# A two-layer hybrid trunk in float32: every dense product in passes of 256 columns at one distance of 180 bytes, decay rows on 128 partitions, block inverses written row by row

## The chip, the cores and the metric

The kernel runs on one core of a Trainium2 chip. The metric is the device time of one execution in microseconds, here the median of three runs. Where a single row is read, it comes from one profiled execution, whose span is a little shorter than the timed runs.

## The reference

The input `x` is 256 tokens of 2048 features, float32. Two layers follow one another, each a mixer and a gated feed-forward with residuals:

```python
# layer 0 mixer: differential attention, 8 heads, two score maps each
qkv = rms_norm(x) @ w_qkv            # 2048 -> 6144
p   = softmax(q k^T - slope * |i - j|)   # q, k normalised per head; chunk mask
x   = x + rms_norm((p1 - lam * p2) @ v) @ w_o
# layer 1 mixer: gated delta rule, 16 key heads, 32 value heads, chunks of 64
q, k, v = silu(causal_conv4(rms_norm(x) @ w_in)); z, beta, g from the same product
a   = I + strict_lower((k * beta) k^T * decay)   # per chunk and head
u   = a^-1 (v * beta); w = a^-1 (k * beta * exp(g))
o_t = q state + (q k^T * decay) (u - w state); state carried from chunk to chunk
x   = x + (rms_norm(o) * silu(z)) @ w_out
# both layers: feed-forward, 5504 hidden columns
u   = causal_conv3(rms_norm(x) @ w_up) + b
x   = x + (silu(gate(u)) * val(u)) @ w_down
```

## The kernel before

Tokens lie on the free axis: `x` and the normalised input `h` are 16 tiles of 128 features by 256 tokens. A float32 operand of a dense product is split into a rounded part and a rest, both of the type `float32r`: `h[k]` holds the two parts side by side (512 columns), and `weights` brings a chunk of four 128x256 weight tiles by DMA from the SP queue into `raw`, has ScalarE round it into `whi` (L89) and VectorE form the rest `wlo` (L90). Three buffers of each rotate. A product is then high x high, low x high and high x low, summed in PSUM.

`dense` does this with the weights as the loaded operand and the activations as the moving one. A step is one 128x128 weight tile and one of the two 128-column halves of the block. By default (L122 to L124) a step has three matmuls of 256 columns each. With `pair=True` it has two: `whi` against both parts of `h` in one matmul of 512 columns (L119), and `wlo` against the first part (L120); the two halves of the 512 columns are added later, in `merge` (L131 to L133) or by a second addition in `add_out` (L243). `pair` holds for the up-projections of both layers (43 blocks of 16 k x 2 steps each, `ffn`) and for the down-projection of layer 0 (8 blocks of 43 x 2 steps, `project`). All others use the default: queries, keys and `w_o` in layer 0, `w_in`, `w_gate` and `w_out` in layer 1, and the last down-projection. `dense_tok` (L148 to L150) has the roles exchanged: activations are loaded and 512 weight columns move. It makes the values of layer 0 (4 blocks) and `z` of layer 1 (8 blocks), each 96 matmuls.

The address at which `whi` and `wlo` start inside their buffers can be shifted by up to 127 elements (`weights(ap, d)`), so that the moving operand and the loaded one stand at a chosen distance modulo 512 bytes. `HP`, `AP` and `OP` are the places of `h`, `ac` and `oc` in such a row of 128 elements. The default products use a distance of 45 elements (180 bytes); the paired ones use one that changes with the block, and `dense_tok` one from the list `TOK`.

Small work is written as generators (`spawn`, `tick`) and mixed between the chunks; the framework's scheduler then sets the order on each engine. In the delta rule (`gdn`) there are four bands of four key heads. For each value head `keys` spreads a row of the decay over 128 partitions by a matmul of `sel` with `rows` on 64 partitions (L486). `invert` computes the inverses of the 32x32 diagonal blocks of a band on VectorE, all 128 partitions at once, into `Ti`, and turns them with two 32x32-block transposes into `ttc` (L543) and `tcc` (L545), laid out as element by matrix (`[partition, i, m]`). `levels` joins them to 64 and 128 rows: GpSimd copies them into `TT` and `Ta` (L558, L560), and TensorE multiplies 32x32 quadrants (L564 with `tcc`, L573 with `ttc`, then L577), twice a band. The trace has two records for each of these float32 matmuls.

Of the kernel before, what the change touches and what calls it, by code (L numbers as in the profile page):

```python
# [8 lines left out]
F32 = mybir.dt.float32  # L9
F32R = mybir.dt.float32r  # L10
# [12 lines left out]
TOK = [x for x in range(64) if x % 4 or x > 32 and x not in (32, 48)]  # L23
# [4 lines left out]
class Trunk:  # L28
# [49 lines left out]
    def weights(self, ap, d=(0, 0)):  # L78
# [8 lines left out]
        raw, hi, lo = tile_("raw", F32, 3), tile_("whi", F32R, 3, P, d[0]), tile_("wlo", F32R, 3, P, d[1])  # L87
# [13 lines left out]
    def dense(self, w, kt, acts, place, tiles=2, lead=0, dist=(45, 45), pair=False):  # L101

# [5 lines left out]
        for k0, nk in self.chunks(kt, CK, lead):  # L108
            hi, lo = self.weights(w[:, k0:k0 + nk, :], [(place - x) % P for x in dist])
# [3 lines left out]
            for k, c in steps:  # L113
# [4 lines left out]
                if pair:  # L118
                    nc.tensor.matmul(ps[:, c, :], hi[:, k, s], a, start=first, stop=False)  # L119
                    nc.tensor.matmul(o, lo[:, k, s], a[:, 0, :], start=False, stop=last)  # L120
                    continue
# [6 lines left out]
    def merge(self, ps, u, pair=False):  # L128

        if pair:  # L130
            self.nc.scalar.copy(u, ps[:, :, T:])  # L131
            self.nc.vector.tensor_tensor(u, ps[:, :, :T], u, ALU.add)
# [4 lines left out]
    def dense_tok(self, w, kt, acts, dists):  # L137
# [3 lines left out]
        for i, (k0, nk) in enumerate(self.chunks(kt, CK // 2)):  # L141
# [97 lines left out]
    def add_out(self, blk, ps, done, pair=False):  # L239

        x = self.x[:, 2 * blk:2 * blk + 2, :]
        for i in range(1 + pair):
            self.nc.vector.tensor_tensor(x, ps[:, :, i * T:(i + 1) * T], x, ALU.add)  # L243
# [5 lines left out]
    def project(self, w, kt, acts, place, done, final=False, pairs=None):  # L249

        n = KD // 2
        for b in range(n):
            ps = self.dense(w[b], kt, acts, place, dist=pairs[b] if pairs else (45, 45), pair=bool(pairs))
            if b < n - final:
                self.add_out(b, ps, done, bool(pairs))
                continue
# [5 lines left out]
    def ffn(self, w_up, w_down, nj, cols_ap, done, final=False):  # L262
# [3 lines left out]
        with self.tc.tile_pool(name="fp", bufs=1) as fp:  # L266
# [5 lines left out]
            for j in range(nj):  # L272
                ps = self.dense(w_up[j], KD, self.h_acts, HP, dist=2 * ((j if not final else 43 + j if j < 21 else 3 * j - 60),), pair=True)
                c = []
                u = fp.tile([P, 2, T], F32, tag="u", name="u", bufs=2)
                self.merge(ps, u, True)
# [11 lines left out]
            self.project(w_down, nj, lambda k: acts[k], AP, done, final, None if final else [(53, 8), (58, 8), (53, 40), (58, 40), (12, 8), (53, 60), (58, 60), (53, 52)])  # L288

    def attention(self, w_qk, w_v, w_o, nh, dist_ap, ident_ap, qg, kg, lvec, sub, start, done, lambda_init):  # L290

        nc, mp = self.nc, self.mp
        with self.tc.tile_pool(name="at", bufs=1) as at:
# [115 lines left out]
            for h in range(0, nh, 2):  # L409
                pv = self.dense_tok(w_v[h // 2], KD, self.h_acts, TOK[2 * h:2 * h + 4])  # L410
# [12 lines left out]
    def gdn(self, w_gate, w_in, w_z, w_out, nb, hb, gate_ap, const_ap, hot_ap, conv_col, ng, done):  # L423
# [12 lines left out]
        with tc.tile_pool(name="gd", bufs=1) as gd:  # L436
# [4 lines left out]
            hot = gd.tile([64, nv], F32, tag="hot", name="hot")  # L441
# [27 lines left out]
            def keys(hq, c, cc, b0, res):  # L469
# [448 lines left out]
```

## Time and profile before

| | |
|---|---|
| time, median of 3 runs | 2720.66 us (2720.05 to 2721.29) |
| profiled execution: its own time is known by its span | 2716.8 us |
| TensorE busy | 2701.9 us (99%), 18912 matmuls |
| VectorE, ScalarE, GpSimd busy | 1909.1, 1489.6, 120.1 us |
| DMA | 481.18 MB, mean 177 GB/s |

By stage, the attention layer takes the first 401 us, the feed-forward of layer 0 lasts to 1125, the delta rule to 1994, the feed-forward of layer 1 to the end at 2717. Busy times are unions over overlapping instructions. Matmuls overlap, so a matmul's own duration is longer than the time that it adds; what it adds is the distance from its start to the next start. In the rows of groups the numbers after the bar are busy time and mean duration of one, then idle time before. In the timeline a row is start, duration, engine, line, operation and tiles (`out<-moving,loaded` for matmuls).

### The profile page before, as it was taken

What the parts mean: (1) busy time and instruction counts of PE and PEld (TensorE: products, weight loads), DVE (VectorE), ACT (ScalarE), POOL (GpSimd) and SP (SyncE); (2) the same over time, 40 slices, a digit from 0 to 9 for tenths busy, and PEclk for the clock granted to TensorE, in tenths of its full rate; (3) what the DMA queues carried; (4) which work ended last, traced back from release to release, by engine and by line L of the source; (5) the groups of instructions that cost most, each with busy time, mean ns of one, the idle gap of its engine ahead of it and who ended that gap; (6) DMA issues with size and microseconds to landing.
All of it is one profiled execution on the core that took longest, in us unless ns stands there. A gap on an engine that the chain in (4) does not pass through costs nothing.

```text
span 2716.8 us, 46973 instructions
## 1 busy us (share of the span) xinstructions
PE 2701.9 (99%) x18912; PEld 2474.2 (91%) x18912; DVE 1909.1 (70%) x2813; ACT 1489.6 (55%) x2077; POOL 120.1 (4%) x220
## 2 busy tenths in 40 slices
PE   8999999999999999999999999999999999999999
PEld 8998898888888888889989989989998888889999
DVE  7775667777777555679687687688677777776444
ACT  6665555555555444574564664574565555555333
POOL 0000000000000000022011011021000000000000
PEclk9999999999999999999999999999999999999999
DMA  6555566666666666655355454455466666666665
GB/s 207 172 171 171 158 200 188 187 190 189 187 187 189 188 189 186 183 158 182 117 162 170 131 169 150 153 164 166 143 193 186 187 188 189 188 188 191 204 200 167
DMA packets 135370, 481.18 MB, mean 177 GB/s; under 512 B 15344, under 2 KB 18416, under 8 KB 135152
## 3 DMA queue, kind: packets, MB, share of 16 engines
q1 hardware_dynamic: 134000, 475.57, 57.9%
q8 instruction: 148, 2.42, 0.4%
q10 hardware_dynamic: 1152, 2.61, 0.3%
q14 instruction: 70, 0.57, 0.1%
HBM read 476.03 MB, written 2.10 MB: 176 GB/s over the span
## 4 chain that ended last, share of the span: by engine, by line
PE 99%; DMA 0%; ACT 0%; DVE 0%; issue 0%; SPq 0%; DVEq 0%; ACTq 0%
PE ps L119 29%; PE ps L120 15%; PE ps L123 13%; PE ps L122 12%; PE ps L124 12%; PE ps L149 3%; PE ps L150 3%; PE ps L148 3%; PE mp L621 2%; PE mp L236 1%; PE mp L509 1%; PE mp L564 0%; PE mp L573 0%; PE mp L486 0%; PE mp L585 0%; PE mp L591 0%
## 5 line engine op out<-in xcount | busy, mean ns | idle before, releaser
L90 DVE TENSOR_TENSOR wlo<-raw,whi 128x1024 fp32r<-128x1024 f32 (+2 forms) x909 | 1108.5, 1221 | 661.5 <-ACT whi L89 658.8
L89 ACT CAST whi<-raw 128x1024 fp32r<-128x1024 f32 (+2 forms) x909 | 947.8, 1043 | 1030.1 <-PE ps L119 430.0
L119 PE MATMUL ps<-h,whi 128*128 128x512 f32 x2752 | 964.9, 394 | 0.0
L120 PE MATMUL ps<-h,wlo 128*128 128x256 f32 x2752 | 772.8, 281 | 0.0
L119 PEld LDWEIGHTS ps<-h,whi 128*128 128x128 f32 x2752 | 516.8, 188 | 120.6
L120 PEld LDWEIGHTS ps<-h,wlo 128*128 128x128 f32 x2752 | 518.3, 188 | 0.0
L122 PE MATMUL ps<-h,whi 128*128 128x256 f32 x1552 | 433.1, 280 | 7.9 <-ACT h L162 5.9
L123 PE MATMUL ps<-h,wlo 128*128 128x256 f32 x1552 | 433.6, 280 | 2.0 <-DVE wlo L90 2.0
L124 PE MATMUL ps<-h,whi 128*128 128x256 f32 x1552 | 432.3, 279 | 0.0
L122 PEld LDWEIGHTS ps<-h,whi 128*128 128x128 f32 x1552 | 292.4, 189 | 10.3 <-ACT h L162 5.9
L123 PEld LDWEIGHTS ps<-h,wlo 128*128 128x128 f32 x1552 | 293.1, 189 | 5.6 <-DVE wlo L90 2.7
L124 PEld LDWEIGHTS ps<-h,whi 128*128 128x128 f32 x1552 | 293.1, 189 | 1.1
L122 PE MATMUL ps<-ac,whi 128*128 128x256 f32 x944 | 260.5, 276 | 0.0
L123 PE MATMUL ps<-ac,wlo 128*128 128x256 f32 x944 | 260.4, 276 | 0.0
L124 PE MATMUL ps<-ac,whi 128*128 128x256 f32 x944 | 260.3, 276 | 0.0
L119 PE MATMUL ps<-ac,whi 128*128 128x512 f32 x688 | 241.8, 395 | 0.0
L120 PE MATMUL ps<-ac,wlo 128*128 128x256 f32 x688 | 193.2, 281 | 0.0
L122 PEld LDWEIGHTS ps<-ac,whi 128*128 128x128 f32 x944 | 177.1, 188 | 0.1
L123 PEld LDWEIGHTS ps<-ac,wlo 128*128 128x128 f32 x944 | 177.1, 188 | 0.0
L124 PEld LDWEIGHTS ps<-ac,whi 128*128 128x128 f32 x944 | 177.1, 188 | 0.0
L119 PEld LDWEIGHTS ps<-ac,whi 128*128 128x128 f32 x688 | 129.5, 188 | 30.8
L148 PE MATMUL ps<-whi,h 128*128 128x512 f32 x384 | 152.8, 398 | 0.0
(211 smaller groups left out, 3418.2 us busy)
## 6 DMA issues: line engine op xcount, KB each, us to landing
raw<-w_up SPq DMA_DIRECT2D x344, 512.0 KB, 4.4
raw<-w_down SPq DMA_DIRECT2D x160, 512.0 KB, 3.8
raw<-w_in SPq DMA_DIRECT2D x128, 512.0 KB, 4.3
raw<-w_z SPq DMA_DIRECT2D x64, 512.0 KB, 3.7
raw<-w_out SPq DMA_DIRECT2D x64, 512.0 KB, 4.0
raw<-w_qk SPq DMA_DIRECT2D x63, 512.0 KB, 4.2
raw<-w_v SPq DMA_DIRECT2D x32, 512.0 KB, 3.6
raw<-w_o SPq DMA_DIRECT2D x32, 512.0 KB, 4.6
```

The source lines that it names most:

```text
L89: nc.scalar.copy(hi, raw)
L90: nc.vector.tensor_tensor(lo, raw, hi.bitcast(F32), ALU.subtract)
L119: nc.tensor.matmul(ps[:, c, :], hi[:, k, s], a, start=first, stop=False)
L120: nc.tensor.matmul(o, lo[:, k, s], a[:, 0, :], start=False, stop=last)
L122: nc.tensor.matmul(o, hi[:, k, s], a[:, 0, :], start=first, stop=False)
L123: nc.tensor.matmul(o, lo[:, k, s], a[:, 0, :], start=False, stop=False)
L124: nc.tensor.matmul(o, hi[:, k, s], a[:, 1, :], start=False, stop=last)
L148: nc.tensor.matmul(ps[:, c, :], ah, hi[:, k, :], start=first, stop=False)
L149: nc.tensor.matmul(ps[:, c, :], ah, lo[:, k, :], start=False, stop=False)
L150: nc.tensor.matmul(ps[:, c, :], al, hi[:, k, :], start=False, stop=last)
L236: last = self.nc.tensor.matmul(out, self.onesr, p[:, j], start=i + j == 0, stop=i + j == n)
L621: nc.tensor.matmul(p[:, v, :], l(v), r[:, v, :], start=i == 0, stop=i == len(terms) - 1)
```

## The change

Three things change.

1. `pair` is gone: every step of `dense` has three matmuls of 256 columns, and every dense product, `dense_tok` too, stands at a distance of 45 elements (`GAP`). In `dense_tok` each 512-column matmul becomes two of 256. `merge` loses two of its three operations in the paired form, `add_out` its second addition.
2. `sel` and the decay `rows` have 128 partitions, of which the upper 64 hold zeros (`hot` is padded with zeros on the way in, GpSimd clears `rows`).
3. `ttc` and `tcc` are laid out as matrix by element (`[partition, m, i]`): the transposes write at a stride, and the matmuls and GpSimd's copies read 32 elements in a row. In `levels` the loop over matrices is outside the loop over the quadrants 0 and 2.

```diff
-TOK = [x for x in range(64) if x % 4 or x > 32 and x not in (32, 48)]
+GAP = 45
...
-    def dense(self, w, kt, acts, place, tiles=2, lead=0, dist=(45, 45), pair=False):
+    def dense(self, w, kt, acts, place, tiles=2, lead=0):
...
-            hi, lo = self.weights(w[:, k0:k0 + nk, :], [(place - x) % P for x in dist])
+            hi, lo = self.weights(w[:, k0:k0 + nk, :], (place - GAP) % P)
...
-                if pair:
-                    nc.tensor.matmul(ps[:, c, :], hi[:, k, s], a, start=first, stop=False)
-                    nc.tensor.matmul(o, lo[:, k, s], a[:, 0, :], start=False, stop=last)
-                    continue
                 nc.tensor.matmul(o, hi[:, k, s], a[:, 0, :], start=first, stop=False)
                 nc.tensor.matmul(o, lo[:, k, s], a[:, 0, :], start=False, stop=False)
                 nc.tensor.matmul(o, hi[:, k, s], a[:, 1, :], start=False, stop=last)
...
-        if pair:
-            self.nc.scalar.copy(u, ps[:, :, T:])
-            self.nc.vector.tensor_tensor(u, ps[:, :, :T], u, ALU.add)
-            self.nc.vector.tensor_tensor(u, u, self.rstd.unsqueeze(1).to_broadcast([P, 2, T]), ALU.mult)
-            return
         self.nc.vector.tensor_tensor(u, ps[:, :, :T], self.rstd.unsqueeze(1).to_broadcast([P, 2, T]), ALU.mult)
...
-            hi, lo = self.weights(w[:, k0:k0 + nk, :], 2 * ((HP + dists[i // 2]) % P,))
+            hi, lo = self.weights(w[:, k0:k0 + nk, :], (HP + GAP) % P)
...
-                    nc.tensor.matmul(ps[:, c, :], ah, hi[:, k, :], start=first, stop=False)
-                    nc.tensor.matmul(ps[:, c, :], ah, lo[:, k, :], start=False, stop=False)
-                    nc.tensor.matmul(ps[:, c, :], al, hi[:, k, :], start=False, stop=last)
+                    halves = [slice(i * T, (i + 1) * T) for i in range(2)]
+                    for j, (l, r) in enumerate(((ah, hi), (ah, lo), (al, hi))):
+                        for i, s in enumerate(halves):
+                            nc.tensor.matmul(ps[:, c, s], l, r[:, k, s],
+                                             start=first and not (i or j), stop=last and i + j == 3)
...
-                    sel = gd.tile([64, P], F32R, tag="sel", name="sel", bufs=2)
-                    nc.gpsimd.tensor_copy(sel, hot[:, h:h + 1].to_broadcast([64, P]))
+                    sel = gd.tile([P, P], F32R, tag="sel", name="sel", bufs=2)
+                    nc.gpsimd.tensor_copy(sel, hot[:, h:h + 1].to_broadcast([P, P]))
...
-                nc.vector.transpose(ttc.rearrange(flat), t.rearrange(flat))
+                nc.vector.transpose(ttc.rearrange("p m i -> p i m"), t)
                 tcc = gd.tile([P, 32, 32], F32, tag="s4", name="tcc", bufs=3)
-                nc.vector.transpose(tcc, t.rearrange("p i c -> p c i"))
+                nc.vector.transpose(tcc.rearrange("p m c -> p c m"), t.rearrange("p i c -> p c i"))
...
-                    nc.gpsimd.tensor_copy(TT[quad[s], :, quad[s]], ttc[quad[s], :, ms].rearrange("p i m -> p m i"))
+                    nc.gpsimd.tensor_copy(TT[quad[s], :, quad[s]], ttc[quad[s], ms, :])
...
-                for s in (0, 2):
-                    for m in range(nm):
+                for m in range(nm):
+                    for s in (0, 2):
                         nc.tensor.matmul(pp[quad[s + 1], m, :], lview[m // 2][quad[s], m % 2, quad[s + 1]],
-                                         tcc[quad[s], :, m0 + m], start=True, stop=True)
+                                         tcc[quad[s], m0 + m, :], start=True, stop=True)
...
-        rows = gd.tile([64, T], F32R, tag="grow", name="grow")
-        nc.scalar.copy(rows, pr)
+        rows = gd.tile([P, T], F32R, tag="grow", name="grow")
+        nc.gpsimd.memset(rows[64:].bitcast(F32), 0.0)
+        nc.scalar.copy(rows[:64], pr)
```

Where the rows of an engine's queue change is best seen at three places. First TensorE, before the change, where layer 0's first up-projection block (`ps_4522`) follows the last block of `w_o` (`ps_4383`); a row is line, operation, out<-moving,loaded and size:

```order
L122 MATMUL ps_4383<-ac_3548,whi_4475 128x256
L123 MATMUL ps_4383<-ac_3548,wlo_4476 128x256
L124 MATMUL ps_4383<-ac_3548,whi_4475 128x256
L119 MATMUL ps_4522<-h_75,whi_4524 128x512
L120 MATMUL ps_4522<-h_75,wlo_4525 128x256
```

The same place after the change (the numbers of tiles differ between the two programs, and `dense`'s three matmuls are now lines 115 to 117):

```order
L115 MATMUL ps_4767<-ac_3932,whi_4859 128x256
L116 MATMUL ps_4767<-ac_3932,wlo_4860 128x256
L117 MATMUL ps_4767<-ac_3932,whi_4859 128x256
L115 MATMUL ps_4906<-h_75,whi_4908 128x256
L116 MATMUL ps_4906<-h_75,wlo_4909 128x256
L117 MATMUL ps_4906<-h_75,whi_4908 128x256
```

The up-projection now goes on in the same pattern as the block ahead of it. The second place is a burst of 32-row products of the third band on TensorE, before; `whi_17408` and `wlo_17409` are the two parts of one weight chunk:

```order
L122 MATMUL ps_17359<-h_75,whi_17408 128x256
L564 MATMUL mp_16876<-tcc_16850,lt_16002 32x32 x2
L564 MATMUL mp_16876<-tcc_16850,lt_16010 32x32 x2
L564 MATMUL mp_16876<-tcc_16850,lt_16187 32x32 x2
L564 MATMUL mp_16876<-tcc_16850,lt_16195 32x32 x2
```

And the same burst after, with the matmuls of two quadrants now side by side:

```order
L115 MATMUL ps_20290<-h_75,whi_20292 128x256
L553 MATMUL mp_19759<-tcc_19721,lt_18741 32x32 x4
L553 MATMUL mp_19759<-tcc_19721,lt_18749 32x32 x4
L553 MATMUL mp_19759<-tcc_19721,lt_18926 32x32 x4
L553 MATMUL mp_19759<-tcc_19721,lt_18934 32x32 x4
L116 MATMUL ps_20290<-h_75,wlo_20293 128x256
```

In both programs the burst stands behind the first matmul of a block's first chunk, whose rest part is the next that VectorE has to form. The third place is VectorE ahead of that burst, before:

```order
L539 TENSOR_TENSOR Ti_16565<-Ti_16565,tmp_16827 128x30
L543 STREAM_TRANSPOSE ttc_16848<-Ti_16565 128x1024
L545 STREAM_TRANSPOSE tcc_16850<-Ti_16565 128x1024
L90 TENSOR_TENSOR wlo_17409<-raw_17407,whi_17408 128x1024
L135 TENSOR_TENSOR u_17347<-ps_17154,rstd_11096 128x512
```

and after:

```order
L90 TENSOR_TENSOR wlo_20239<-raw_20237,whi_20238 128x1024
L207 SCALAR_TENSOR_TENSOR cv_20074<-u_20072,cols_79,cv_20074 128x253 x2
L532 STREAM_TRANSPOSE ttc_19719<-Ti_19316 128x32x32
L534 STREAM_TRANSPOSE tcc_19721<-Ti_19316 128x32x32
L90 TENSOR_TENSOR wlo_20293<-raw_20291,whi_20292 128x1024
```

The transposes keep their place between two weight splits; the split behind them, `wlo_17409` before and `wlo_20293` after, is the one that TensorE needs right behind the burst.

More of the change, by code (lines that the diff above doesn't have):

```diff
@@ L237, in total, with add_out @@
         return last
-    def add_out(self, blk, ps, done, pair=False):
+    def add_out(self, blk, ps, done):
         x = self.x[:, 2 * blk:2 * blk + 2, :]
-        for i in range(1 + pair):
-            self.nc.vector.tensor_tensor(x, ps[:, :, i * T:(i + 1) * T], x, ALU.add)
+        self.nc.vector.tensor_tensor(x, ps[:, :, :T], x, ALU.add)
         if done:
@@ L247, in add_out, with project @@
             self.add_squares()
-    def project(self, w, kt, acts, place, done, final=False, pairs=None):
+    def project(self, w, kt, acts, place, done, final=False):
         n = KD // 2
         for b in range(n):
-            ps = self.dense(w[b], kt, acts, place, dist=pairs[b] if pairs else (45, 45), pair=bool(pairs))
+            ps = self.dense(w[b], kt, acts, place)
             if b < n - final:
-                self.add_out(b, ps, done, bool(pairs))
+                self.add_out(b, ps, done)
                 continue
@@ L272, in ffn @@
             for j in range(nj):
-                ps = self.dense(w_up[j], KD, self.h_acts, HP, dist=2 * ((j if not final else 43 + j if j < 21 else 3 * j - 60),), pair=True)
+                ps = self.dense(w_up[j], KD, self.h_acts, HP)
                 c = []
                 u = fp.tile([P, 2, T], F32, tag="u", name="u", bufs=2)
-                self.merge(ps, u, True)
+                self.merge(ps, u)
                 for half in range(2):
@@ L570, in levels @@
                 px = small(32)
-                for s in (0, 2):
-                    for m in range(nm):
-                        nc.tensor.matmul(px[quad[s], m, :], pc[quad[s + 1], m, :], ttc[quad[s + 1], :, m0 + m],
+                for m in range(nm):
+                    for s in (0, 2):
+                        nc.tensor.matmul(px[quad[s], m, :], pc[quad[s + 1], m, :], ttc[quad[s + 1], m0 + m, :],
                                          start=True, stop=True)
@@ L843, in _layout @@
         "const": np.concatenate(const, 1).astype(f),
-        "hot": np.concatenate([np.eye(NV)] * 2).astype(f),
+        "hot": np.concatenate([np.eye(NV)] * 2 + [np.zeros((P - 2 * NV, NV))]).astype(f),
         "w_up1": blocks(x["ffn_w_up"][1], KD, up),
```

22 lines of the change are left out of this document (11 added, 11 removed).

## The prediction

> **What bounds the kernel now.** I read the page's head and its chain of waits first, then the list of TensorE's waits, then the busy time by stage.
>
> ```profile
> span 2716.8 us, 46973 instructions
> ...
> PE 99%; DMA 0%; ACT 0%; DVE 0%; issue 0%; SPq 0%; DVEq 0%; ACTq 0%
> ```
>
> ```profile
> PE ps L122 <- ACT h L162: 5.9, 1, 5.9
> PE ps L123 <- DVE wlo L90: 2.0, 3, 1.2
> PE ps L122 <- ACT whi L89: 2.0, 1, 2.0
> PE mp L730 <- DVE glin L726: 1.2, 1, 1.2
> ```
>
> The chain is TensorE at 99%, and TensorE waits 11.1 us in all (total, times, longest in each row), nearly all of it at the start and at the entry of the delta-rule layer. So the time is the sum of the distances from one matmul's start to the next one's, and the question is what each kind of matmul adds to that sum. A row's duration (276 to 400 ns) is no help, because matmuls overlap; starts and counts are. The stages of the two feed-forward layers give both. The windows below are up-projection of layer 0, its down-projection, up-projection of layer 1, its down-projection; the first number after the window is its length in us, then come TensorE's busy time and matmuls, its weight loads, VectorE, ScalarE, GpSimd, and last the granted clock, the DMA share and GB/s.
>
> ```profile
> 401.60:883.80 482.20, 482.20 (x2760) 422.39 (x2759) 362.89 (x518) 276.52 (x389) 0.00 (x0) 1.00 0.62 189
> 883.90:1125.50 241.60, 241.60 (x1377) 210.87 (x1376) 126.65 (x137) 101.99 (x121) 0.00 (x0) 1.00 0.63 183
> ...
> 1994.70:2478.80 484.10, 484.10 (x2760) 423.04 (x2759) 363.48 (x518) 276.34 (x389) 0.00 (x0) 1.00 0.62 188
> 2478.90:2712.70 233.80, 233.80 (x2065) 233.80 (x2064) 110.98 (x101) 90.74 (x91) 0.00 (x0) 1.00 0.66 193
> ```
>
> The two down-projections do the same arithmetic (8 blocks of 43 x 2 steps). The first does a step in a pass of 512 and a pass of 256 columns (1376 matmuls, 241.60 us, 351 ns a step); the last does it in three passes of 256 at 180 bytes (2064 matmuls, 233.80 us, 113.3 ns a pass, 340 ns a step). The clock column is 1.00 in all four. This pair is the main evidence: the form that the change brings everywhere is already there, 7.8 us shorter for the same work.
>
> **The change, part by part.**
>
> *Feed-forward steps.* 43 x 32 + 8 x 86 + 43 x 32 = 3440 steps take 482.20 + 241.60 + 484.10 = 1207.9 us. After it they are 10320 passes at 113.3 ns, 1169.2 us, and the 16 records of the norms inside the two up windows stay (a pass each, 1.8 us). Gain 36.9 us. The built program has moving minus stationary address at 180 modulo 512 bytes in every dense matmul, with the same buffers as before, so nothing but the passes differs from the last window. What goes with it on the other engines is off the path:
>
> ```profile
> L132 DVE TENSOR_TENSOR u<-ps,u 128x512 f32<-128x512 f32 x86 | 58.8, 684 | 0.0
> L131 ACT COPY u<-ps 128x512 f32<-128x512 f32 x86 | 49.9, 580 | 0.0
> ```
>
> Both go (as does one of two additions at `add_out` in layer 0's down-projection, 8 of some 0.69 us); the multiply by `rstd` stays and reads PSUM. I cost this at nothing, as TensorE has no row waiting for `u`. The cover that must hold is that weights keep up with shorter blocks: VectorE was busy 362.89 of 482.20 us in the first window and needs 43 x 0.68 less in about 469; DMA moved 193 GB/s in the last window, the pace now asked of the up windows, without a wait of TensorE. Would the cover go, up blocks would stay at some 350 ns a step and the 36.9 would shrink to the 7.7 of the down-projection.
>
> *Token-major products* (`dense_tok`: values in layer 0, `z` in the delta rule; 12 blocks of 96 passes of 512 columns become 192 of 256). Two stretches with nothing else on TensorE:
>
> ```profile
> 273.90:290.55 16.65, 16.65 (x75) 13.51 (x74) 10.37 (x14) 9.44 (x15) 0.00 (x0) 1.00 0.57 167
> ...
> 1816.80:1847.84 31.04, 31.04 (x135) 24.97 (x133) 27.31 (x52) 12.24 (x13) 3.22 (x8) 1.00 0.63 190
> ```
>
> Three of each count stand across the edges, so 16.65/72 = 231 and 31.04/132 = 235 ns a pass; I take 233.2. 1152 passes are 268.6 us. After: 2304 passes. No row has them, since here the weights move and the activations are loaded; the bounds are 113.3 (above) and 120 ns (rows further down). I take 113.3, as the moving address again lies 180 bytes above the loaded one and each pass again has one weight load: 261.0 us, gain 7.6 us (at 120: a loss of 7.9).
>
> *Decay rows.* `sel` x `rows` on 64 partitions, 32 times (one for each value head). Beside it, a 128-partition matmul of the same type among passes:
>
> ```profile
> 39.58 0.28 PE L123 MATMUL ps<-h,wlo 128*128 128x256 f32 x1
> 39.69 0.39 PE L236 MATMUL mp<-sqp,onesr 128*128 128x512 f32 x1
> 39.93 0.28 PE L124 MATMUL ps<-h,whi 128*128 128x256 f32 x1
> 40.04 0.28 PE L122 MATMUL ps<-h,whi 128*128 128x256 f32 x1
> ```
>
> ```profile
> 1171.80 0.28 PE L124 MATMUL ps<-h,whi 128*128 128x256 f32 x1
> 1172.01 0.38 PE L486 MATMUL mp<-grow,sel 64*128 64x256 f32 x1
> 1172.32 0.38 PE L122 MATMUL ps<-h,whi 128*128 128x256 f32 x1
> 1172.54 0.28 PE L123 MATMUL ps<-h,wlo 128*128 128x256 f32 x1
> ```
>
> The full-height one slips in at pass speed (39.58 to 40.04: two passes and twice 256 columns). The half-height one makes gaps of 0.21, 0.31 and 0.22 us around it: 0.74 us where three passes take 0.35. 32 x 0.39 = 12.5 us gained; the bounds are 0 (if the gaps have another cause) and 12.5, and I take the upper, since number type, columns and neighbours are alike and only the height differs. GpSimd's wider copies, the zeros in 64 rows and the larger `hot` load are off TensorE's queue; nothing waits for GpSimd there.
>
> *Block inverses.* The 32-row products read `tcc` and `ttc` at a stride of 32 elements, one row quadrant after the other; after, they read 32 elements in a row and alternate quadrants. Each of 8 bursts (4 bands, 2 groups):
>
> ```profile
> 1657.86 0.28 PE L122 MATMUL ps<-h,whi 128*128 128x256 f32 x1
> 1658.06 1.75 PE L564 MATMUL mp<-tcc,lt 32*32 32x32 f32 x32
> 1659.74 0.39 PE L123 MATMUL ps<-h,wlo 128*128 128x256 f32 x1
> ```
>
> ```profile
> 1287.69 1.58 PE L573 MATMUL mp<-ttc,pc 32*32 32x32 f32 x29
> ...
> 1289.10 0.23 PE L573 MATMUL mp<-ttc,pc 32*32 32x32 f32 x1
> 1289.11 0.22 PE L577 MATMUL mp<-pc,TT 32*32 32x32 f32 x2
> 1289.16 0.23 PE L573 MATMUL mp<-ttc,pc 32*32 32x32 f32 x1
> 1289.17 0.22 PE L577 MATMUL mp<-pc,TT 32*32 32x32 f32 x2
> ...
> 1289.23 0.51 PE L577 MATMUL mp<-pc,TT 32*32 32x32 f32 x11
> 1289.67 0.38 PE L122 MATMUL ps<-h,whi 128*128 128x256 f32 x1
> ```
>
> L564: first to last start 1.75 - 0.23 = 1.52 us for 32, 48 ns each. L577, contiguous on one quadrant: (0.51 - 0.19)/10 = 32 ns. Two quadrants at once (1289.10 to 1289.16): three starts in 60 ns, 20 each. I take 22, 0.70 us a burst, saving 0.8 x 8 = 6.6 us (at 32 ns: 4.0; at 16: 8.1). L573 with L577 behind it lasts 1.98 us (1287.69 to 1289.67); 0.70 + 16 x 0.032 + 0.12 = 1.33, saving some 0.6 x 8 = 4.9. Together 11.5 us, bounds 0 (stride and order cost nothing) and 14.6. The price is on VectorE, which writes these tiles:
>
> ```profile
> 1654.03 1.25 DVE L543 STREAM_TRANSPOSE ttc<-Ti 128x1024 f32<-128x1024 f32 x1
> 1655.20 2.09 DVE L545 STREAM_TRANSPOSE tcc<-Ti 128x1024 f32<-128x1024 f32 x1
> ```
>
> A strided input costs 0.84 us. Strided output has no row; if it costs as much, the first gets 0.84 longer and the second as much again. `tcc` ended at 1657.29, the burst began at 1658.06: 0.77 us of cover, and queued behind the transposes is the weight split for the next chunk. At most both double, +3.3 us, 2.5 beyond the cover in 4 bands: 0 to 10 us; I take 1 us, nearest to the strided-input row. GpSimd's copies into `TT` and `Ta` get contiguous reads and end no later. The scheduler moved a few bursts (rows of the order, above): I count three more interruptions by half- or quarter-height work, at the 0.2 us of such an entry (1657.86 to 1658.06), 0.5 us.
>
> *Sum.* 36.9 + 7.6 + 12.5 + 11.5 - 1.0 - 0.5 = 67.0 us, against the profiled span of 2716.8: 2649.8. The median of the runs is 2720.7, 3.9 above the span; with that, 2653.7 us. The 11.1 us of waits stay.
>
> **The rivals.** *A 256-column pass costs more than half of a 512-column one everywhere* (a fixed part per matmul, paid 4592 times more). For it speaks an up block of layer 1:
>
> ```profile
> 2030.13 0.39 PE L119 MATMUL ps<-h,whi 128*128 128x512 f32 x1
> 2030.36 0.28 PE L120 MATMUL ps<-h,wlo 128*128 128x256 f32 x1
> 2030.48 0.40 PE L119 MATMUL ps<-h,whi 128*128 128x512 f32 x1
> ```
>
> 0.12 after 0.23. At 118 ns a pass the feed-forward would take 11.7 us more and the token products 3.3 more; with the 22.5 of the other parts, 2713.2 us. Against it is the last window's 113.3. The Trainium skill ("TensorE: Matmul & The Clock Gate", section "Wait — 56ns, not 53.3ns?") speaks for this rival: it gives each warm matmul its columns over the clock plus a fixed 2.5 ns. By its figures three passes of 256 would be 2.5 ns longer than 512 + 256, an estimate of 11.5 us lost over 4592 splits, and about 2709.7 us; the windows disagree with it, 340 against 351 ns a step.
>
> *Slower: the passes fall into a slower rhythm.* Eight passes in the delta rule, no other work between:
>
> ```profile
> 1541.72 0.28 PE L124 MATMUL ps<-h,whi 128*128 128x256 f32 x1
> ...
> 1542.68 0.28 PE L123 MATMUL ps<-h,wlo 128*128 128x256 f32 x1
> ```
>
> 0.96/8 = 120 ns at the very same 180 bytes: there is a second rhythm, entered after other work. Should the up blocks enter it and stay, 10320 x 0.120 = 1238.4 us: 32.3 lost, 7.9 with the token products, 22.5 gained: 2738.4 us. It decides from (1207.9 + 268.6 + 22.5 - 1.8)/12624 = 118.6 ns a pass. Against it: the last window kept 113.3 for 234 us.
>
> *Only the token products* take 120: 2669.2. *Bursts no shorter*: 2665.2. *VectorE becomes the bound while it inverts* (27.31 of 31.04 us busy above, and longer transposes): up to 9 us more, 2662.7.
>
> **How the numbers follow.** The sum as worked out: 0.70, with a range of its own of 2646 to 2661 (bursts at their ends, transposes free or covered). Token products at 120: 0.09. Bursts no shorter: 0.07. VectorE: 0.05. Fixed part per matmul: 0.04. Slower rhythm: 0.03; 0.02 for what I don't see. 2643 to 2676 takes in all but the last three and leaves a little below for the slow rhythm leaving the delta rule. A measurement can tell about 0.2%, 5.4 us: faster 0.93 (the first four cases and half of the fixed part), within it 0.03 (the other half, where it meets bursts or token products that don't gain, and 0.01 unseen), slower 0.04 (the slow rhythm, 0.01 unseen).
>
> **What would show it.** Right: up windows near 469 us with 4136 matmuls, both down-projections alike at 234; token stretches at 113 ns; no gaps of 0.2 to 0.3 us around the `sel` matmul; 32-row bursts near 0.7 us; waits still near 11 us. Wrong: 118 to 120 ns in the up windows, rows of TensorE waiting for `wlo` or `tcc`, or bursts still at 48 ns a start.

## The result and the profile after

The changed kernel takes 2675.01 us (median of 4 runs, 2674.91 to 2676.33), the kernel before 2720.36 beside it (4 runs): a ratio of 0.983, interval 0.982 to 0.985. The forecast was 2653.7, in a range of 2643 to 2676: the direction and most of the steps were right, but 45 us came instead of 67, and the time lies 1 us inside the slow end of the range.

The profiled execution has a span of 2674.6 us (2716.8 before). These are the windows of the changed kernel by stage: attention, up- and down-projection of layer 0, the delta-rule layer, up- and down-projection of layer 1. The first number after the window is its length; the columns are those of the windows before.

```profile
0.00:405.20 405.20, 395.73 (x3296) 391.59 (x3297) 269.50 (x401) 236.59 (x379) 0.20 (x4) 1.00 0.57 178
405.20:874.00 468.80, 468.80 (x4137) 468.75 (x4136) 334.83 (x476) 256.65 (x347) 0.00 (x0) 1.00 0.64 194
874.00:1107.90 233.90, 233.90 (x2066) 233.90 (x2065) 121.66 (x129) 101.48 (x120) 0.00 (x0) 1.00 0.65 190
1107.90:1967.80 859.90, 855.03 (x7814) 842.50 (x7813) 672.98 (x1135) 511.94 (x711) 111.94 (x217) 1.00 0.52 160
1967.80:2436.60 468.80, 468.80 (x4137) 468.75 (x4136) 335.12 (x476) 256.43 (x347) 0.00 (x0) 1.00 0.64 194
2436.60:2670.50 233.90, 233.90 (x2066) 233.90 (x2064) 110.38 (x100) 90.25 (x90) 0.00 (x0) 1.00 0.67 193
```

The feed-forward layers gave what was forecast, 482.20 to 468.80, 241.60 to 233.90 and 484.10 to 468.80. What is missing is in the two other windows: the delta rule went from 868.9 to 859.9 us only, and attention got longer, 401.6 to 405.2. In attention 3.2 of these 3.6 us are the products of the values, 89.9 to 93.1 us, which were split like `z`.

What happened in the delta rule can be seen in two neighbouring stretches with almost nothing but passes in them. The first is the second `z` block (192 token-major passes), the second the two dense blocks behind it (2 x 96 passes):

```profile
1205.79:1228.83 23.04, 23.04 (x195) 23.04 (x193) 20.36 (x39) 9.57 (x10) 0.00 (x0) 1.00 0.61 194
1228.83:1251.87 23.04, 23.04 (x195) 23.04 (x193) 21.05 (x38) 10.91 (x13) 2.93 (x5) 1.00 0.52 161
```

23.04/192 = 120.0 ns a pass in both. The token products run at 120 and not at 113.3, which was one of the rivals. And the dense blocks behind, which have the distance of 180 bytes that gave 113.3 in the feed-forward layers, go on at 120 until other work interrupts them. The timeline of TensorE shows this at a burst of the third band:

```profile
1634.57 0.28 PE L117 MATMUL ps<-h,whi 128*128 128x256 f32 x1
1634.69 0.28 PE L115 MATMUL ps<-h,whi 128*128 128x256 f32 x1
1634.90 0.69 PE L553 MATMUL mp<-tcc,lt 32*32 32x32 f32 x32
1635.52 0.38 PE L116 MATMUL ps<-h,wlo 128*128 128x256 f32 x1
1635.74 0.28 PE L117 MATMUL ps<-h,whi 128*128 128x256 f32 x1
1635.86 0.28 PE L115 MATMUL ps<-h,whi 128*128 128x256 f32 x1
1635.98 0.28 PE L116 MATMUL ps<-h,wlo 128*128 128x256 f32 x1
1636.09 0.28 PE L117 MATMUL ps<-h,whi 128*128 128x256 f32 x1
```

Starts 0.12 apart ahead of the burst, 0.11 and 0.12 in turn (113) soon behind it. Nine dense blocks behind `z` blocks took 11.52 us instead of 10.88. The same rows show the burst of 32 matmul records (two to a matmul) at 0.69 us (1.75 before): first to last start 0.69 - 0.19 = 0.50 us, 16 ns each.

Around the `sel` matmul of the decay rows, now on 128 partitions, the gaps are gone:

```profile
1175.94 0.28 PE L117 MATMUL ps<-h,whi 128*128 128x256 f32 x1
1176.06 0.28 PE L475 MATMUL mp<-grow,sel 128*128 128x256 f32 x1
1176.17 0.28 PE L115 MATMUL ps<-h,whi 128*128 128x256 f32 x1
```

The transposes on VectorE, by line, both with strided output now, and the waits of TensorE (in all, times, longest):

```profile
L534 DVE STREAM_TRANSPOSE tcc<-Ti 128x1024 f32<-128x1024 f32 x4 | 8.6, 2158 | 0.0
L532 DVE STREAM_TRANSPOSE ttc<-Ti 128x1024 f32<-128x1024 f32 x4 | 8.4, 2091 | 0.0
```

```profile
PE ps L115 <- ACT h L152: 5.6, 1, 5.6
PE ps L116 <- DVE wlo L90: 4.4, 6, 1.4
PE ps L115 <- ACT whi L89: 2.0, 2, 1.1
PE ps L139 <- DVE wlo L90: 1.0, 1, 1.0
```

A strided output costs what a strided input cost (1.25 to 2.09 us), and strided on both sides costs hardly more than on one (2.16). The waits for `wlo` are larger than before (5.4 us with both rows, 2.0 before).

To divide the delta-rule layer, each start-to-start distance of TensorE was put to the matmul that began it, and of each 256 columns of a dense or token product 113.3 ns were counted as its normal cost. What is above it is "pace" in an undisturbed run of passes, "edge" next to other work, and "stall" where it is long (16 ns and more above 113.3 for 256 columns). In us:

| delta rule | before | after | after, token products in 512 |
|---|---|---|---|
| pace, dense | 3.2 | 8.7 | 5.4 |
| pace, token | 5.0 | 10.3 | 5.0 |
| edges, dense and token | 16.8 | 13.8 | 12.4 |
| stalls, dense and token | 0.6 | 6.6 | 2.6 |
| decay rows, bursts, all other small work | 141.6 | 118.6 | 117.6 |

The small work gained what was forecast, and 16.8 us of pace and stalls gave two thirds of it back.

### The profile page after: what moved, and what is told of

Its sections match the earlier page's. It is cut to its first block, busy times and chain, and to the rows that moved or that the text cites. A ratio compares the mean times of both kernels' runs of the same rounds, so it can differ in the third digit from the quotient of the medians.

```text
span 2674.6 us, 55978 instructions
## 1 busy us (share of the span) xinstructions
PE 2656.4 (99%) x23504; PEld 2639.4 (99%) x23504; DVE 1845.2 (69%) x2719; ACT 1453.3 (54%) x1994; POOL 112.1 (4%) x221
## 4 chain that ended last, share of the span: by engine, by line
PE 93%; DVE 3%; ACT 3%; issue 1%; DMA 1%; ACTq 0%; DVEq 0%; SPq 0%
PE ps L115 26%; PE ps L116 26%; PE ps L117 26%; PE ps L139 10%; PE mp L610 2%; DVE wlo L90 1%; ACT whi L89 1%; PE mp L226 1%; DVE cv L207 1%; ACT L455 0%; PE mp L574 0%; PE mp L580 0%; DMA raw<-w_in 0%; PE mp L589 0%; PE mp L498 0%
## 5 line engine op out<-in xcount | busy, mean ns | idle before, releaser
L115 PE MATMUL ps<-h,whi 128*128 128x256 f32 x4304 | 1195.0, 278 | 7.8 <-ACT h L152 5.6
L117 PE MATMUL ps<-h,whi 128*128 128x256 f32 x4304 | 1193.7, 277 | 0.0
L115 PEld LDWEIGHTS ps<-h,whi 128*128 128x128 f32 x4304 | 809.4, 188 | 9.8 <-ACT h L152 5.6
L117 PEld LDWEIGHTS ps<-h,whi 128*128 128x128 f32 x4304 | 810.0, 188 | 0.6
L115 PE MATMUL ps<-ac,whi 128*128 128x256 f32 x1632 | 450.4, 276 | 0.0
L117 PE MATMUL ps<-ac,whi 128*128 128x256 f32 x1632 | 450.2, 276 | 0.0
L116 PEld LDWEIGHTS ps<-ac,wlo 128*128 128x128 f32 x1632 | 306.2, 188 | 0.0
L139 PE MATMUL ps<-whi,h 128*128 128x256 f32 x1536 | 251.1, 284 | 0.0
L139 PEld LDWEIGHTS ps<-whi,h 128*128 128x128 f32 x1536 | 213.5, 190 | 0.2
L139 PE MATMUL ps<-wlo,h 128*128 128x256 f32 x768 | 155.7, 284 | 1.0 <-DVE wlo L90 1.0
L115 PE MATMUL ps<-oc,whi 128*128 128x256 f32 x512 | 143.9, 281 | 0.0
L207 DVE SCALAR_TENSOR_TENSOR cv<-u,fcols,cv 128x255 f32<-128x255 f32 (+1 forms) x344 | 142.8, 477 | 0.0
L117 PE MATMUL ps<-oc,whi 128*128 128x256 f32 x512 | 142.5, 278 | 0.0
L116 PE MATMUL ps<-oc,wlo 128*128 128x256 f32 x512 | 142.3, 278 | 0.0
```

Source lines behind the costliest of these rows:

```text
L115: nc.tensor.matmul(o, hi[:, k, s], a[:, 0, :], start=first, stop=False)
L117: nc.tensor.matmul(o, hi[:, k, s], a[:, 1, :], start=False, stop=last)
L139: nc.tensor.matmul(ps[:, c, s], l, r[:, k, s], start=first and not (i or j), stop=last and i + j == 3)
L207: nc.vector.scalar_tensor_tensor(out[:, j:], u[:, :T - j], taps[n - 1 - j], out[:, j:], ALU.mult, ALU.add)
```

## The experiments

**Token products in 512-column passes.** The changed kernel, with `dense_tok` and its list of distances as before.

```
-  hi, lo = self.weights(w[:, k0:k0 + nk, :], (HP + GAP) % P)
+  hi, lo = self.weights(w[:, k0:k0 + nk, :], (HP + dists[i // 2]) % P)
...
-  for i, s in enumerate(halves):
-      nc.tensor.matmul(ps[:, c, s], l, r[:, k, s],
-                       start=first and not (i or j), stop=last and i + j == 3)
+  nc.tensor.matmul(ps[:, c, :], ah, hi[:, k, :], start=first, stop=False)
+  nc.tensor.matmul(ps[:, c, :], ah, lo[:, k, :], start=False, stop=False)
+  nc.tensor.matmul(ps[:, c, :], al, hi[:, k, :], start=False, stop=last)
```

> The changed kernel with one part undone: the token-major products (values, z) again in passes of 512 columns at their old list of distances. Theory 'rhythm': in the changed kernel the token passes run at 120 ns a 256-column pass and the dense blocks that follow z keep that rhythm. Then the token blocks fall from 280.8 us to about 271.5, the blocks behind z fall from 11.52 to 10.88 us each (9 blocks, 5.8 us), and the time is about 2660 us. Theory 'order' (the lost time of the delta rule lies in the scheduler's new order and VectorE's longer transposes): the token blocks gain their 9 us, the blocks behind z stay at 11.52, about 2666 us.

2657.24 us, ratio to before 0.976 (0.975 to 0.978): 17.8 us less than the changed kernel. The token products fell from 280.8 to 269.8 us (271.5 before the change), all nine dense blocks behind `z` blocks took 10.88 to 10.92 us again, and, not expected, the stalls fell from 6.6 to 2.6 us (the table). So the split of the token products costs some 18 us in all: 9 in themselves without their stalls, 3 in the dense blocks behind, 4 in stalls, and the rest in small work and edges.

**A distance for each block.** All products in 256-column passes, but up block `j` at `j` elements in layer 0 and at `43 + j` in layer 1, and the token blocks at 12 distances.

```
-  hi, lo = self.weights(w[:, k0:k0 + nk, :], (place - GAP) % P)
+  hi, lo = self.weights(w[:, k0:k0 + nk, :], (place - gap) % P)
...
+  ps = self.dense(w_up[j], KD, self.h_acts, HP, gap=j + 43 * final)
```

> The changed kernel with its distance swept: up-projection block j of layer 0 at j elements (0 to 42), of layer 1 at 43+j (43 to 85), all in passes of 256 columns; the 12 token blocks at 3, 7, 83, 27 (values) and 39, 0, 16, 64, 96, 109, 31, 15 elements (z). Theory 'distance decides': up blocks differ by distance, 10.88 us at 45 and up to 11.5 (120 ns a pass) at others, and some token blocks reach 113 to 114 ns a pass, where those at 45 had 120. Theory 'width decides': all up blocks stand within 1% of 10.88 us whatever the distance, and all token blocks at about 120, since it is the moving of the weights that costs. Under 'distance' the whole is slower than the changed kernel, some 2675 to 2710 us; under 'width' 2675.

2711.75 us (one run), a little above the expected range. Windows of up blocks at 12, 13 and 14 elements in layer 0, at 45, and at 76, 77 and 78 in layer 1:

```profile
540.45:551.65 11.20, 11.20 (x99) 11.20 (x98) 7.84 (x11) 5.92 (x8) 0.00 (x0) 1.00 0.59 190
551.65:562.53 10.88, 10.88 (x98) 10.88 (x97) 7.76 (x11) 5.92 (x8) 0.00 (x0) 1.00 0.58 194
562.53:574.05 11.52, 11.52 (x99) 11.52 (x97) 7.76 (x11) 5.91 (x8) 0.00 (x0) 1.00 0.57 185
2007.30:2018.19 10.89, 10.89 (x98) 10.89 (x97) 7.78 (x11) 5.94 (x8) 0.00 (x0) 1.00 0.57 190
...
2359.01:2370.21 11.20, 11.20 (x99) 11.20 (x97) 7.84 (x11) 5.92 (x8) 0.00 (x0) 1.00 0.57 188
2370.21:2381.09 10.88, 10.88 (x98) 10.88 (x97) 7.75 (x11) 5.92 (x8) 0.00 (x0) 1.00 0.59 191
2381.09:2392.61 11.52, 11.52 (x98) 11.52 (x97) 7.85 (x11) 5.91 (x8) 0.00 (x0) 1.00 0.58 186
```

Only 13, 42, 45, 51 and 77 gave 10.9 us (113 ns a pass); the next best has 11.11, the middle of the 86 blocks is 11.36 and the slowest 11.73. The pattern repeats after 64 elements (256 bytes): of the 22 distances that have a partner 64 further on, 21 agree within 0.01 us. So 180 bytes is one of few good places, and most others would have made the feed-forward layers slower than before: 73 of the 86 blocks are above the mean of 11.22 us that the paired form had.

That it is the distance, and not the place of the weights in their own row of 128 elements, the down-projections show. There 45 elements put the weights at place 3 (`AP` is 48), and their passes take 113.3 ns. In this scan the block at 37 elements has the weights at the same place 3 (`HP` is 40), and it is the slowest of all, 11.73 us.

Of the 12 token blocks none came below 116.7 ns. Behind the second `z` blocks at 0 and 109 elements the dense blocks were carried along at 120, behind those at 64 and 15 they were not. The one at 64 elements had 120 ns a pass itself, so the pace ahead does not decide alone (first this `z` block, then the dense block behind it):

```profile
1396.06:1419.08 23.02, 23.02 (x194) 23.02 (x193) 18.91 (x37) 9.54 (x10) 1.02 (x4) 1.00 0.56 176
1419.08:1429.97 10.89, 10.89 (x98) 10.89 (x97) 9.98 (x18) 5.38 (x6) 0.00 (x0) 1.00 0.59 182
```

**Paired passes, all at 45 elements.** The kernel before, with one edit:

```
-  dist=2 * ((j if not final else 43 + j if j < 21 else 3 * j - 60),), pair=True)
+  dist=(45, 45), pair=True)
```

> The kernel before with its up blocks still in a pass of 512 and a pass of 256 columns, but all at 45 elements instead of a distance for each block. Theory 'width and distance only work together': the one paired block at 45 in the kernel before took 11.30 us against a mean of 11.22, so 86 blocks take some 7 us more, 2727 us. Rival 'the distance alone gave the gain of the feed-forward layers': paired blocks settle at 10.9 us when all share 45, 2692 us.

2727.88 us (one run; 2718.54 before beside it). One up block of each layer:

```profile
414.33:425.64 11.31, 11.31 (x67) 9.99 (x65) 9.71 (x16) 7.69 (x10) 0.00 (x0) 1.00 0.58 184
...
2024.56:2035.87 11.31, 11.31 (x67) 9.95 (x65) 8.45 (x12) 6.42 (x9) 0.00 (x0) 1.00 0.62 186
```

11.31 us, as nearly all of the 86, and as the one such block before (11.30). With the run above that makes a square of four, in means of a block: pairs at many distances 11.22 us, pairs at 45 11.31, single passes at many distances 11.36, single passes at 45 10.88. Neither the width nor the distance gains anything alone; each alone loses, and together they gain 0.34 us a block.

**Loop orders of the token products.** Twelve token blocks with an order (which of token half, column half and product runs innermost) and a distance each.

```
+  for c, j, i in sorted(((c, j, i) for c in range(2) for j in range(3) for i in range(2)), key=loops):
```

> Twelve token blocks of 192 passes of 256 columns, each with a loop order and a distance of its own. Theory 'repeated load': a pass is slowed because the next one loads the same 128 columns of the activations again; then the blocks in which the two token halves alternate innermost (every pass loads other columns than the one before) run at 113.3 ns, 21.8 us a block at 45 elements, and the others at 120 ns, 23.0 us. Theory 'distance': the order is indifferent and only the distance modulo 512 bytes between what is moved and what is loaded decides, with other good values than where the weights are loaded; then every block at 45 stays at 120 ns (23.0 us) in all orders, every block at 15 has about 116.7 ns (22.4 us), and the two at 13 and 51, which are good for dense blocks, say whether the good values are shared (21.8 us) or not. Whole kernel about 2670 us if only the halves-alternating blocks gain, 2673 if only the distances do.

2668.68 us (one run). The second `z` blocks of the four bands: product innermost at 45; the original order at 15; the original order at 13; the original order at 51:

```profile
1204.21:1227.25 23.04, 23.04 (x194) 23.04 (x193) 20.33 (x39) 9.57 (x10) 0.00 (x0) 1.00 0.62 193
1374.01:1396.42 22.41, 22.41 (x195) 22.41 (x194) 18.89 (x36) 9.54 (x10) 0.99 (x4) 1.00 0.56 178
1584.16:1607.21 23.05, 23.05 (x194) 23.05 (x193) 20.82 (x40) 9.56 (x10) 0.00 (x0) 1.00 0.62 200
1794.43:1817.05 22.62, 22.62 (x194) 22.62 (x193) 21.08 (x39) 9.55 (x10) 0.00 (x0) 1.00 0.62 207
```

At 45 elements every order has its passes at 120 to 123 ns, also the one in which each pass loads other columns than the one ahead; at 15 the three orders tried have 116.7 to 117. So the repeated load is not the cause, and the distance decides. But 13, 45 and 51, where dense blocks have 113, have 120, 120 and 118 here: the good places are not shared. The dense blocks were carried along at 120 behind the first of these four `z` blocks alone, not behind the one at 13, which had 120 as well; that and the faster blocks at 15 took the time below the 2673 us that was expected of this outcome.

**All distances for the token products.** The 96 distances that are no multiple of 4, each for one chunk of 24 passes.

```
+  ODD = [x for x in range(128) if x % 4]
...
-  hi, lo = self.weights(w[:, k0:k0 + nk, :], (HP + GAP) % P)
+  hi, lo = self.weights(w[:, k0:k0 + nk, :], (HP + ODD[8 * blk + i]) % P)
```

> The changed kernel with a distance of its own for each of the 96 chunks of 24 passes in the token blocks: all distances from 1 to 127 elements that are no multiple of 4, once each. Theory 'the role decides': with the activations loaded and the weights moved, 256-column passes have good distances of their own; then some chunks run at 113 to 114 ns a pass (2.72 us a chunk), others at 120 and above. Rival 'the width is wrong for this form': none gets below about 116 ns, and passes of 512 (227 ns, twice 113.5) stay the better form of the token products. Whole kernel 2668 to 2680 us either way.

2668.53 us (one run). The chunk at 45, and two of the better ones, 59 and 59 + 64:

```profile
1181.65:1184.53 2.88, 2.88 (x26) 2.88 (x25) 2.88 (x6) 2.85 (x5) 2.65 (x6) 1.00 0.22 43
1215.61:1218.42 2.81, 2.81 (x27) 2.81 (x25) 2.71 (x5) 1.05 (x1) 0.00 (x0) 1.00 0.64 214
1805.34:1808.15 2.81, 2.81 (x26) 2.81 (x25) 2.71 (x5) 1.05 (x1) 0.00 (x0) 1.00 0.69 230
```

The median pass of a chunk lies between 117 and 123 ns, with 120 in the middle, and again the list repeats after 64 elements (46 of 48 partners within 1 ns). No distance reaches 113: for this form the width was wrong, not the place. Multiples of 4 were not all tried (0, 16, 64 and 96 had medians of 118 to 120 ns in the run with a distance for each block). The last chunk of each second `z` block had 120 ns a pass here, at 63, 85, 106 and 127 elements, and behind none of the four were the dense blocks carried along (10.88 to 10.93 us).

**Token products in 512 at the four best distances.** The first experiment, with the list of distances cut to four.

```
-  TOK = [x for x in range(64) if x % 4 or x > 32 and x not in (32, 48)]
+  TOK = [7, 15, 27, 39] * 12
```

> The changed kernel with the token products in passes of 512 columns, and only at the distances 7, 15, 27 and 39 elements, which took 227 ns a pass in the kernel before, against 233 for the mean of its list. Theory 'rhythm': 1152 passes x 6.2 ns = 7.1 us less than with the whole list (2657.2 us): 2650 us, no dense block behind a z block above 10.9 us. Rival: the 227 ns belong to the neighbours that those passes had (other work between, other dense blocks ahead), not to the distance; then 2657 us as with the whole list.

2651.61 us (5 runs, 2650.07 to 2655.57), ratio to before 0.975 (0.974 to 0.977). It beats both kernels. The second `z` block and the two dense blocks behind it, the stretches that took 23.04 us each:

```profile
1198.15:1220.03 21.88, 21.88 (x98) 18.00 (x97) 20.27 (x40) 9.56 (x10) 0.00 (x0) 1.00 0.67 208
1220.03:1241.79 21.76, 21.76 (x193) 21.72 (x192) 20.36 (x43) 11.03 (x13) 0.00 (x0) 1.00 0.61 191
```

228 ns for 512 columns, and 113.3 for the dense passes behind. The token products take 265.0 us in all (269.8 with the whole list): 4.8 us less, of the 7.1 expected. A further 1.8 us is in the pace of the dense passes of the delta rule.

**Decay rows back on 64 partitions.**

```
-  sel = gd.tile([P, P], F32R, tag="sel", name="sel", bufs=2)
+  sel = gd.tile([64, P], F32R, tag="sel", name="sel", bufs=2)
...
-  rows = gd.tile([P, T], F32R, tag="grow", name="grow")
-  nc.gpsimd.memset(rows[64:].bitcast(F32), 0.0)
+  rows = gd.tile([64, T], F32R, tag="grow", name="grow")
```

> The changed kernel with the decay rows and sel on 64 partitions again. If the half height makes the gaps around the sel matmul, they come back, 0.42 us each, 32 times: 13 us, about 2688 us. If the gain came from the changed order around them, the gaps stay small and the time stays within 5 us of 2675.

2683.40 us (2681.88 to 2684.28), 8.4 more. TensorE's timeline has the gaps again:

```profile
1538.02 0.38 PE L475 MATMUL mp<-grow,sel 64*128 64x256 f32 x1
1538.33 0.38 PE L117 MATMUL ps<-h,whi 128*128 128x256 f32 x1
1538.55 0.28 PE L115 MATMUL ps<-h,whi 128*128 128x256 f32 x1
```

By the division above, small work and edges got 10.1 us longer, and the stalls 3.6 us shorter; attention, which the edit does not touch, happened to be 1.3 us shorter in the profiled execution. The profiled spans differ by 5.5 us. So the height is worth 10.1 us by itself, and less in the total. That the stalls shrink because the gaps give the weight chunks time fits this, but is not shown.

**Block inverses as before.** Old tiles, strided reads, one row quadrant after the other, transposes as before.

```
-  nc.vector.transpose(ttc.rearrange("p m i -> p i m"), t)
+  nc.vector.transpose(ttc.rearrange(flat), t.rearrange(flat))
...
-  for m in range(nm):
-      for s in (0, 2):
+  for s in (0, 2):
+      for m in range(nm):
```

> The changed kernel with the block inverses laid out element by matrix again and the quadrants one after the other. The 32-row bursts should cost 15.7 us more (29.2 instead of 13.5). If VectorE's longer transposes cause the waits of TensorE for wlo in the delta rule (about 4 us), these go and the time is about 2687 us; if the order causes them, they stay and it is about 2691 us.

2692.91 us (2691.13 to 2694.61), 17.9 more; the delta-rule layer is 15.9 longer, nearly all of it in the 32-row products (13.5 to 29.2 us). TensorE's waits in this kernel:

```profile
PE ps L116 <- DVE wlo L90: 4.5, 6, 1.4
PE ps L115 <- ACT whi L89: 1.8, 2, 1.1
```

They are as large as with the longer transposes, and so are the stalls (6.3 us against 6.6). So the longer transposes do not cause the waits.

**The two halves of that edit.** Contiguous reads, but the quadrants one after the other:

```
-  for m in range(nm):
-      for s in (0, 2):
+  for s in (0, 2):
+      for m in range(nm):
```

> The changed kernel with the 32-row products on one row quadrant after the other again, as before, but reading 32 elements in a row. Theory 'both parts matter': a start every 32 to 33 ns instead of 48.6 (before) and 21.1 (mean after): 640 x 33 = 21 us in these bursts against 13.5 after, whole kernel about 2682.6 us. Rival: the contiguous reads alone give all of it, 2675 us; or the alternation alone does, then the bursts are back at 29 us and the kernel at 2691.

And the old tiles with strided reads, but the quadrants in turn:

```
-  nc.vector.transpose(tcc.rearrange("p m c -> p c m"), t.rearrange("p i c -> p c i"))
+  nc.vector.transpose(tcc, t.rearrange("p i c -> p c i"))
...
-                   tcc[quad[s], m0 + m, :], start=True, stop=True)
+                   tcc[quad[s], :, m0 + m], start=True, stop=True)
```

> The changed kernel with the old tiles (32-row products read at a stride of 128 bytes, transposes written as before), but with the two row quadrants alternating. If two quadrants overlap whatever they read, a strided start costs half of 48.6: 512 x 24.3 + 4.3 = 16.7 us in these bursts, about 2678 us. If the stride is a limit that the quadrants share, 29 us and 2691 us.

2682.92 and 2681.66 us (one run each). The same burst of the third band in both, first with the contiguous reads alone, then with the alternation alone:

```profile
1638.89 1.09 PE L553 MATMUL mp<-tcc,lt 32*32 32x32 f32 x32
```

```profile
1637.05 1.07 PE L553 MATMUL mp<-tcc,lt 32*32 32x32 f32 x32
```

1.75 us with neither, 1.09 and 1.07 with one, 0.69 with both. Over all 640 products it is 29.2, 19.6, 19.6 and 13.5 us: each half gives 9.6 us alone, the second adds 6.1. Alternating strided reads is dearer than half of one quadrant's (29.8 ns a start in the mean of the 512 strided ones, where 24.3 was the estimate), which speaks for the stride being partly a limit that the quadrants share. The Trainium skill ("TensorE: Matmul & The Clock Gate", section "The mechanism" of Part 3) states that a weight load overlaps running matmuls only if it goes to another row group; the step from 1.09 to 0.69 us by alternation alone is in line with that, but does not single it out, since the column group of the output alternates too. For full-height passes this trace does not agree: all are on the same rows, and yet weight loads are busy for 2639.4 and matmuls for 2656.4 of the 2674.6 us, so loads run beside matmuls nearly all the time.

## Why the prediction came out as it did

*What bounds the kernel.* Right: TensorE is the chain, 99% busy, and the sum of its start-to-start distances gave every term.

*Feed-forward steps, -36.9 us:* measured -36.3 (the four windows). Taking the pace from the last window, 113.3 ns, was right, and so was the cover: no wait of TensorE in these windows. The rival of a fixed part per matmul is refuted: three passes at 45 take 340 ns and a pair at 45 takes 353 (11.31 us/32). With it the rule of the Trainium skill ("TensorE: Matmul & The Clock Gate", section "Wait — 56ns, not 53.3ns?") finds no support here, since a constant per matmul can't make the order of the two forms turn with the distance, as the square of four shows.

*Token products, -7.6 us:* this is the step that failed. They got 9.3 us longer (271.5 to 280.8), of which 2 are stalls. The step took 113.3 because "the moving address again lies 180 bytes above the loaded one". The scans show that this is not enough: with activations loaded and weights moved, 45 elements gives 120, and no distance tried gives 113. The bound of 120 was the right end, and the rival with it came true; but its time, 2669.2 us, was 5.8 us too low, since the next item was not in it either.

*What no step had.* A slow pace is carried into the dense blocks behind (pace of dense passes 3.2 to 8.7 us, 5.5 more). The prediction knew a "second rhythm, entered after other work", priced it only for the up blocks, and costed the delta rule's dense blocks at nothing. They were not free: they stand behind the token products, and the nine blocks entered the slow pace with no other work in between and left it at the next such work. With the token products back at 512 columns these nine are fast again, so the split of the token products causes it.

*Decay rows, -12.5:* from the start of the matmul ahead of `sel` to that of the second behind it are 787 ns in the mean of 32 in the changed kernel with 64 rows and 427 with 128 (the step had 0.74 and 0.35 us), 11.5 us; over all small work and edges 10.1. Mechanism and size were right, a little of it is lost next to other work.

*Block inverses, -11.5, bounds 0 to 14.6:* -15.7, more than the upper bound. The step took 22 ns a start from three starts on two quadrants of a mixed row; the burst measured 16, and the first products gained 8.4 us instead of 6.6. The second and third gained 7.3 instead of 4.9.

*Transposes +1 and interruptions +0.5:* the transposes got longer as the price said (1.25 to 2.09 us) and the stalls of TensorE in the delta rule rose by 6.0 us, but the old transposes leave them as they are. At one stall of 1.0 us (behind the TensorE start at 1327.31) ScalarE and VectorE show why the chunk was late. The rows of the timeline are ScalarE's, then VectorE's:

```profile
1322.12 1.28 ACT L194 ACT_TABLE_LOAD   x1 [2.89 <-DVE os L634]
...
1323.74 1.28 ACT L194 ACT_TABLE_LOAD   x1
...
1326.07 1.05 ACT L89 CAST whi<-raw 128x1024 fp32r<-128x1024 f32 x1
```

```profile
1327.15 1.23 DVE L90 TENSOR_TENSOR wlo<-raw,whi 128x1024 fp32r<-128x1024 f32 x1 [2.91 <-ACT whi L89]
```

ScalarE's queue waited 2.89 us for a row sum and loaded two tables, and the cast of the next weights stood behind them; VectorE, idle, waited for the cast, and TensorE for VectorE. That the chunks are late since blocks are shorter is in line with the runs (with 512-column token products or the gaps of the decay rows the stalls fall to about 3 us), but deeper weight buffers, which would test it, were not tried: this cause is argued, not shown.

*The sum.* In us against the span: -36.3 feed-forward, +8.6 pace of the token products, +5.5 carried pace, +6.0 stalls, -10.1 decay rows, -15.7 inverses, together -42.0; the span fell by 42.2. The terms are taken between two profiled executions, while the times are medians: the profiled execution of the changed kernel took 2676.33 us, the longest of its four, with 1.7 us outside its span, and the medians differ by 45.3. So the 3.9 us added for what lies around the span were for the most part the difference between one execution and the median.

*Inside the range by luck.* The range left room for token products at 120 (2669.2 us), not for the carried pace and the stalls. That the time stayed 1 us below its end is owed to the inverses, which gained 4.2 us more than the sum had, and to the 3.5 us by which the 3.9 were too much: without either it would have been outside.

## What to carry to other kernels

A pace measured for one form of product holds for that form: when operands change roles, scan the distance again, with the very width that will be used, before costing hundreds of blocks by it. When a slow stretch of matmuls stands ahead of a fast one, allow for the fast one being slow up to the next interruption, and look in the trace whether it is. And a gain on the bounding engine takes away cover: look at which queue forms the next operands, and what stands ahead of them there.

## What the runs showed of the hardware

The pace of 256-column passes depends on the distance between moved and loaded operand with a period of 256 bytes (21 of 22 dense partners within 0.01 us a block, 46 of 48 token partners within 1 ns a pass), from 113 to 122 ns for dense passes (11.73 us/96) and 117 to 123 for token passes. Why the two forms differ at the same distance stays open. In the token passes `h` was loaded from one place throughout, so there the distance and the place of the weights are not told apart. The pace can have a memory: at the same distance and the same buffers nine blocks ran at 120 ns behind token blocks of 120, and at 113 soon behind a burst of other work. But behind `z` blocks at 64 and 13 elements, which took 23.02 and 23.05 us (120 ns a pass too), dense blocks had 10.88 to 10.92 us; what decides whether a pace is carried on stays open. Of 32-row matmuls, counted by records, two row quadrants in turn start one every 16 ns in the mean of a burst, one quadrant one every 31 to 32 with contiguous reads, and one every 49, again in the mean, at a stride of 128 bytes.
